# Reading values and gates from the projection's PSUM bank instead of from an SBUF copy

## The chip, the cores and the metric

The kernel runs on one core of a Trainium2 chip. The metric is the device time of one execution in microseconds (us), taken as the median of three runs. The engines are named as the profile names them: PE is TensorE's matmul, PEld its weight load, ACT is ScalarE, DVE is VectorE, POOL is GpSimd and SP the engine that issues the DMAs. SBUF is the on-chip working memory; PSUM holds the matmul results in banks of 512 float32 per partition. POOL does not read PSUM anywhere in this kernel, before or after.

## The reference

Two layers over x of 2048 frames by 1024 columns. Each layer normalizes x, makes one wide projection, splits its columns into q, k, v and gate g for two groups of heads, attends, multiplies each head's output by silu(g), concatenates, projects and adds the residual:

```python
z = rms_norm(x, ln_g) @ w_in
aq, ak, av, ag, bq, bk, bv, bg, bf = split_cols(z, EVEN_SPLITS)
aq = rms_norm(aq.reshape(bsz, seq, A_HEADS, 2, HEAD_DIM), a_qn_g)
...
mixed = jnp.concatenate([a_out * jax.nn.silu(ag), b_out * jax.nn.silu(bg)], axis=-1)
return x + mixed @ w_out
```

Layer 0 has A, four heads of differential attention over all earlier 64-frame chunks (two softmaxes, the second subtracted with a learned weight), and B, eight heads of causal attention with a forget bias. Layer 1 has C, eight query heads over two key-value heads in a window, and D, eight heads over the own and eight earlier chunks. Only q and k are RMS-normalized per head; v and g are used as the projection leaves them.

## The kernel before

The work is cut into steps. A step is one head unit and one block of 128 frames (tb, 0 to 15). The units follow one another: four units of A, four of B (each two heads), the output projection of layer 0, two units of C, four of D, the output projection of layer 1. In the trace these stages lie at about 0 to 780 us (A), 780 to 1430 (B), 1430 to 1620 (output projection), 1620 to 1990 (C, its first unit to 1820), 1990 to 2440 (D) and 2440 to the end.

One step of A, B or D does this:

- PE makes z, 128 frames by 512 columns (128 each of q, k, v, g), with 24 matmuls (`proj`, L242 to L244): eight blocks of the contraction, each as high x high, high x low and low x high of float16 pairs. z lies in one PSUM bank; the pool of these banks, `pz`, has two (`bufs` 2), shared by z, by C's key-value projection zk and by the output projections' zo.
- `evac` (L248) has ACT copy z into the SBUF tile zs, times a power of two held per partition in `sc`. Afterwards nothing reads the bank, and PE may fill it again, two projections later.
- `qk_prep` (L253) squares q and k (ACT, L258), sums (DVE, L260), takes the inverse root (`rstd`, L115: POOL L119 and the power on POOL L121, then DVE L123 to L125), scales q and k (DVE L266), applies k's gain (POOL L269), splits into float16 high and low parts (ACT L272, POOL L273). PE transposes them (L277, L281), ACT copies the results out as kT and qT (L283, L286).
- `v_split` (L289) multiplies zs's value columns by another power of two (POOL L294) and splits them: high part on ACT (L109), low part on POOL (L113).
- `silu2` (L308) takes tanh of the gate columns of zs on ACT (L313), forms (1 + tanh) x g on DVE (L314) and multiplies by a factor on POOL (L316, or L318 for A, where the factor is the row `subg`).
- QK products go to another PSUM pool (L339), DVE adds the bias and takes the running extreme (L351), ACT takes exp (L374), `weights_T` splits the weights (ACT L302, DVE L303), a DMA transposes them into pT, and PE multiplies them with V (L407; L497 for A). In A the second softmax is combined into the first by DVE (L484) and POOL (L481, L482).

In C's first unit a step makes two projections: zk with 256 columns (k and v, `post2`), then z with 512 (four heads of q, 256 gate columns). In its second unit a step makes only z.

Python code writes the pieces of a step in a merged order (`drive`): the projection of the step two ahead, the transposes of the step one ahead, QK of this one, the weighted sums of the last two. A scheduler then orders each engine's instructions over the whole program, so a change of a few instructions moves others too. Each engine works its queue strictly in that order: an instruction that waits holds up all that stand behind it.

Of the kernel before, what the change touches and what calls it, by code (L numbers as in the profile page):

```python
# [9 lines left out]
F32 = mybir.dt.float32  # L10
# [4 lines left out]
AF = mybir.ActivationFunctionType  # L15
ALU = mybir.AluOpType
AX = mybir.AxisListType

P = 128
# [40 lines left out]
class Trunk:  # L60
    def __init__(self, ctx, tc, t):
        self.ctx, self.tc, self.nc, self.t = ctx, tc, tc.nc, t
        nc = self.nc
        pool = lambda name, bufs, **k: ctx.enter_context(tc.tile_pool(name=name, bufs=bufs, **k))
        self.const = pool("const", 1)
        self.wp = pool("wp", 11)
        self.xp = pool("xp", 4)
        self.kvp = pool("kvp", 1)
        self.ap = pool("ap", 1)
        self.sm = pool("sm", 6)  # L70
        self.wsc = pool("wsc", 8)
        self.dram = pool("dram", 1, space=bass.MemoryType.DRAM)
        self.pz = pool("pz", 2, space=bass.MemoryType.PSUM)
        self.pS = pool("pS", 2, space=bass.MemoryType.PSUM)
        self.pT = pool("pT", 1, space=bass.MemoryType.PSUM)
        self.pO = pool("pO", 1, space=bass.MemoryType.PSUM)

        self.idf = self.const.tile([P, P], F32, name="idf")
        one = self.const.tile([P, 1], F32, name="one")
        nc.vector.memset(one[:], 1.0)  # L80
        nc.scalar.activation(one[:], one[:], AF.Exp)
        make_identity(nc, self.idf[:])
        self.lng = []
        for i in range(2):
            g = self.const.tile([P, KB], F32, name=f"lng{i}")
            nc.sync.dma_start(g[:], t[f"ln{i}"])
            self.lng.append(g)
        self.idh = self.const.tile([P, P], F16, name="idh")
        nc.vector.tensor_copy(self.idh[:], self.idf[:])
        self.onesf = self.const.tile([P, P], F32, name="onesf")  # L90
        nc.vector.memset(self.onesf[:], 1.0)
        self.mhalf = self.const.tile([P, 8], F32, name="mhalf")
        nc.vector.memset(self.mhalf[:], -0.5)

        def dt_(n, s):
            return [self.dram.tile(s, F32, name=f"{n}{b}") for b in range(NT)]

        self.xs = [[self.dram.tile([P, 2 * KB * P], F16, name=f"xs{i}_{b}") for b in range(NT)] for i in range(2)]
        self.xT = [[None] * NT for _ in range(2)]
        self.mix = [dt_("mixa", [P, DM]), dt_("mixb", [P, DM])]  # L100
        self.x1 = dt_("x1_", [P, DM])
        self.cumd = [self.dram.tile([8, 512], F32, name=f"cumd{i}") for i in range(4)]
# [143 lines left out]


    def evac(self, z, n, sc):  # L248
        zs = self.ap.tile([P, 512], F32, tag="zs", name="zs", bufs=3)
        self.nc.scalar.activation(zs[:, :n], z[:, :n], AF.Copy, scale=sc[:, 0:1])  # L250
        return zs

# [33 lines left out]
            nc.scalar.activation(qT[:].rearrange("p n a t -> p (n a) t"), pt[:, :2 * nq], AF.Copy)  # L286
            st["q"] = [qT[:, s] for s in range(nq)]

    def v_split(self, z, sc, heads):  # L289

        nc = self.nc
        V = self.kvp.tile([P, heads, 2, P // heads], F16, tag="V", name="V", bufs=19)
        z = z.rearrange("p (h d) -> p h d", h=heads)
        nc.gpsimd.tensor_scalar(out=z, in0=z, scalar1=sc[:, 1:2], scalar2=1.0, op0=ALU.mult, op1=ALU.mult)  # L294
        self.split(V[:, :, 0], V[:, :, 1], z, nc.scalar, nc.gpsimd)
        return V

    def weights_T(self, w, n, scale=PSC):
# [6 lines left out]
        nc.sync.dma_start_transpose(out=pt[:, :2 * n // P], in_=hl[:, :2 * n])  # L305
        return pt[:, :2 * n // P].rearrange("p (a b) q -> p a b q", a=2)

    def silu2(self, z, mul):  # L308

        nc = self.nc  # L310
        n = z.shape[1]
        g = self.ap.tile([P, n], F32, tag="gate", name="gate", bufs=7)
        nc.scalar.activation(g[:], z, AF.Tanh, scale=0.5)  # L313
        nc.vector.scalar_tensor_tensor(out=g[:], in0=g[:], scalar=1.0, in1=z, op0=ALU.add, op1=ALU.mult)  # L314
        if mul.shape[1] == 1:
            nc.gpsimd.tensor_scalar(out=g[:], in0=g[:], scalar1=mul, scalar2=1.0, op0=ALU.mult, op1=ALU.mult)  # L316
        else:
            nc.gpsimd.tensor_tensor(out=g[:], in0=g[:], in1=mul, op=ALU.mult)  # L318
        return g
# [106 lines left out]
    def unit_A(self, h, W, wsc, X):  # L426
        nc, ap = self.nc, self.ap
        ks, vs = [], []

        def mk(tb):  # L430
            st = {}
            m = tb + 1

            def p():
                def z():
                    if "z" not in st:
                        st["z"] = self.pz.tile([P, 512], F32, tag="z", name="z")
                    return st["z"][:]
                pieces = self.proj(st, z, W, 512)
                if h == 0:  # L440
                    pieces.append((KB * 0.056, lambda: self.forget(st)))

                def post():
                    z = self.evac(st["z"], 512, wsc())
                    kd = self.ktile(ks, tb)
                    g = self.qk_prep(st, z, 2, 2, self.gA[h], kd)
                    if h == 0:
                        self.forget_gate(st, tb)
                    next(g)
                    vs.append(self.v_split(z[:, 256:384], wsc(), 1))  # L450
                    st["gate"] = self.silu2(z[:, 384:512], self.subg[:])
                    next(g)
                    st["fin"] = g
                return pieces + [(0.34, post)]
# [62 lines left out]
    def unit_BD(self, kind, u, W, wsc, X):  # L517
        nc, ap = self.nc, self.ap
# [16 lines left out]
        def mk(tb):  # L535
            st = {}
# [3 lines left out]
            def p():  # L540
                def z():
                    if "z" not in st:
                        st["z"] = self.pz.tile([P, 512], F32, tag="z", name="z")
                    return st["z"][:]
                pieces = self.proj(st, z, W, 512)

                def post():
                    z = self.evac(st["z"], 512, wsc())
                    kd = self.ktile(ks, tb)
                    g = self.qk_prep(st, z, 2, 2, self.gB if kind == "B" else self.gD, kd)  # L550
                    next(g)
                    vs.append(self.v_split(z[:, 256:384], wsc(), 2))
                    st["gate"] = self.silu2(z[:, 384:512], wsc()[:, 2:3])
                    next(g)
                    st["fin"] = g
                    prep(tb)
                return pieces + [(0.34, post)]
# [46 lines left out]
    def unit_C(self, kv, W, wsc, Wkv, wsckv, KV, X):  # L604
# [6 lines left out]
        def mk(tb):  # L611
# [6 lines left out]
            def p():  # L618
                def zf(k):
                    if k not in st:  # L620
                        st[k] = self.pz.tile([P, 512], F32, tag="z", name="z")
                    return st[k]
                pieces = []
                if Wkv is not None:
                    def post2():
                        z2 = self.evac(st["zk"], 256, wsckv())
                        kd = self.ktile(ks, tb)
                        g = self.qk_prep(st, z2, 0, 2, self.gC, kd)
                        next(g)
                        vs.append(self.v_split(z2[:, 128:256], wsckv(), 2))  # L630
                        next(g)
                        st["fink"] = g
                    pieces = self.proj(st, lambda: zf("zk")[:, :256], Wkv, 256)
                    pieces.append((0.11, post2))

                def post():
                    z = self.evac(st["z"], 512, wsc())
                    g = self.qk_prep(st, z, 4, 0, self.gC, None, self.islope[:, 4 * kv:4 * kv + 4])
                    next(g)
                    st["gate"] = self.silu2(z[:, 256:512], usc[0]()[:, 2:3])  # L640
                    next(g)
                    st["fin"] = g
                return pieces + self.proj(st, lambda: zf("z")[:], W, 512) + [(0.45, post)]
# [271 lines left out]
    def run(self):  # L915
# [23 lines left out]
        def squares(key, kb, raw=None):  # L939

            src, n = parts(key, kb)
            if kb == 0:
                scales[key] = self.sm.tile([P, KB], F32, tag="wss", name="wss", bufs=2)
            g = gains(key)
            junk = raw
            if raw is None:
                raw = junk = self.wp.tile([P, 512], F32, tag="wrn", name="wrn", bufs=1)[:, :n]
                nc.sync.dma_start(raw, src)
            else:
                junk = self.ap.tile([P, 512], F32, tag="zs", name="junk", bufs=3)[:, :n]  # L950
            self.w_squares(scales[key][:, kb:kb + 1], raw, None if g is None else g[:, kb:kb + 1], junk)
            if kb == KB - 1:
                scales[key] = self.w_scale(scales[key][:], None if g is None else g[:])
# [187 lines left out]
```

## Time and profile before

| | |
|---|---|
| median of 3 runs | 2637.18 us (2636.54 to 2644.25) |
| the profiled execution's own time | 2638.93 us |
| its span, first to last instruction | 2637.2 us |
| mean granted PE clock | 0.961 |
| busy share: PE, DVE, ACT, POOL | 89%, 70%, 71%, 55% |

Busy is time in which an engine has an instruction running. Matmuls overlap, so PE's share overstates how near it is to its limit: a 128x512 matmul is shown with about 380 ns, but where PE is not held up the next one starts 215 ns later. "Idle before" counts what an engine stood still ahead of a kind of instruction, and names what it waited for. The times in a timeline are from the span's start.

### The profile page before, as it was taken

What the parts mean: (1) busy time and instruction counts of PE and PEld (TensorE: products, weight loads), DVE (VectorE), ACT (ScalarE), POOL (GpSimd) and SP (SyncE); (2) the same over time, 40 slices, a digit from 0 to 9 for tenths busy, and PEclk for the clock granted to TensorE, in tenths of its full rate; (3) what the DMA queues carried; (4) which work ended last, traced back from release to release, by engine and by line L of the source; (5) the groups of instructions that cost most, each with busy time, mean ns of one, the idle gap of its engine ahead of it and who ended that gap; (6) DMA issues with size and microseconds to landing.
All of it is one profiled execution on the core that took longest, in us unless ns stands there. A gap on an engine that the chain in (4) does not pass through costs nothing.

```text
span 2637.2 us, 53573 instructions
## 1 busy us (share of the span) xinstructions
PE 2345.4 (89%) x18560; PEld 1295.5 (49%) x18560; DVE 1851.6 (70%) x5212; ACT 1861.5 (71%) x4289; POOL 1453.8 (55%) x2311
## 2 busy tenths in 40 slices
PE   6779888989899989898986988999989999998899
PEld 3335444545455555455543434665555454555444
DVE  6877899798886867768676444666777676667431
ACT  6777677777777878778787444778888777777420
POOL 4647777786785645546463001756475757575300
PEclk9889999999999999999997999999999999999899
DMA  7875645355456997979789999345566676756982
GB/s 224 194 173 150 137 110 127 84 127 115 99 128 131 195 185 159 205 151 190 159 170 219 275 276 251 98 94 145 127 172 147 161 143 156 153 127 135 254 229 94
DMA packets 888208, 426.68 MB, mean 162 GB/s; under 512 B 785376, under 2 KB 816096, under 8 KB 887936
## 3 DMA queue, kind: packets, MB, share of 16 engines
q1 hardware_dynamic: 887936, 423.27, 70.1%
q8 instruction: 145, 2.38, 0.4%
q14 instruction: 127, 1.04, 0.1%
HBM read 187.68 MB, written 42.01 MB: 87 GB/s over the span
## 4 chain that ended last, share of the span: by engine, by line
PE 23%; DMA 13%; ACT 10%; DVE 9%; POOL 8%; issue 7%; SPq 1%; POOLq 0%; ACTq 0%; DVEq 0%
DMA pT<-ph 6%; PE z L242 3%; PE z L243 3%; PE z L244 3%; PE zo L242 2%; PE OT L407 2%; PE pss L339 2%; PE zo L243 2%; PE zo L244 2%; DVE row L351 2%; ACT ph L302 2%; POOL y L121 2%; DVE ph L303 2%; ACT row L374 2%; DMA wrn<-in_wd_dram 1%
## 5 line engine op out<-in xcount | busy, mean ns | idle before, releaser
L374 ACT ACTIVATE row<-row,mx 128x1024 f32<-128x1024 f32 (+7 forms) x512 | 438.2, 857 | 118.7 <-DVE mx L351 117.0
L339 PE MATMUL pss<-kT,qT 128*128 128x512 f16 (+3 forms) x1728 | 398.7, 347 | 50.4 <-DVE mx L351 38.9
L242 PE MATMUL z<-w,xr 128*128 128x512 f16 x896 | 346.7, 388 | 23.2 <-DMA xr<-xhl 14.0
L303 DVE SCALAR_TENSOR_TENSOR ph<-row,ph 128x1024 f16<-128x1024 f32 (+6 forms) x320 | 286.6, 905 | 106.2 <-ACT ph L302 104.8
L242 PE MATMUL z<-w,x 128*128 128x512 f16 x896 | 344.4, 384 | 7.1 <-DMA x<-xs 6.7
L243 PE MATMUL z<-w,xr 128*128 128x512 f16 x896 | 346.4, 387 | 3.8 <-POOL w L113 2.4
L244 PE MATMUL z<-w,xr 128*128 128x512 f16 x896 | 345.5, 386 | 0.0
L243 PE MATMUL z<-w,x 128*128 128x512 f16 x896 | 344.4, 384 | 0.0
L244 PE MATMUL z<-w,x 128*128 128x512 f16 x896 | 344.1, 384 | 0.0
L121 POOL TENSOR_TENSOR y<-v,mhalf 128x4 f32<-128x4 f32 (+2 forms) x329 | 306.5, 933 | 9.4
L407 PE MATMUL OT<-V,pT 128*128 128x64 f16 x5688 | 236.0, 196 | 82.5 <-DMA pT<-ph 79.4
L407 PEld LDWEIGHTS <-pT 128*128 128x128 f16 x5688 | 214.4, 100 | 149.5 <-DMA pT<-ph 104.1
L302 ACT ACTIVATE ph<-row 128x1024 f16<-128x1024 f32 (+6 forms) x320 | 234.3, 744 | 52.5 <-DMA pT<-ph 49.0
L339 PEld LDWEIGHTS <-qT 128*128 128x128 f16 x1728 | 153.3, 101 | 173.6 <-issue 58.5
L273 POOL TENSOR_TENSOR hl<-zs,hl 128x256 f16<-128x256 f32 (+1 forms) x240 | 179.9, 750 | 103.3 <-ACT hl L272 100.5
L123 DVE TENSOR_TENSOR q<-y 128x4 f32<-128x4 f32 (+2 forms) x329 | 92.3, 281 | 197.4 <-POOL y L121 195.5
L272 ACT ACTIVATE hl<-zs 128x512 f16<-128x512 f32 (+1 forms) x240 | 145.7, 608 | 54.4 <-POOL zs L269 47.9
L250 ACT ACTIVATE zs<-z,sc 128x512 f32<-128x512 f32 (+1 forms) x240 | 157.8, 660 | 33.9 <-PE z L244 33.4
L242 PE MATMUL zo<-w,xm 128*128 128x512 f16 x352 | 139.0, 395 | 29.3 <-DMA xm<-mhl 12.4
L242 PEld LDWEIGHTS <-xr 128*128 128x128 f16 x960 | 95.4, 99 | 117.3 <-DMA xr<-xhl 15.1
L113 POOL TENSOR_TENSOR w<-wraw,w 128x512 f16<-128x512 f32 x118 | 145.6, 1236 | 13.6 <-ACT w L109 12.6
L286 ACT ACTIVATE qT<-ptq 128x512 f16<-128x512 f16 (+1 forms) x224 | 144.8, 647 | 8.0 <-PE ptq L281 6.8
(223 smaller groups left out, 5489.1 us busy)
## 6 DMA issues: line engine op xcount, KB each, us to landing
x<-xs SPq DMA_DIRECT2D x112, 512.0 KB, 3.8
wraw<-in_w_dram SPq DMA_DIRECT2D x64, 256.0 KB, 3.0
wrn<-in_w_dram SPq DMA_DIRECT2D x56, 256.0 KB, 2.9
x<-in_x_dram SPq DMA_DIRECT2D x16, 512.0 KB, 4.9
xs<-xt SPq DMA_DIRECT2D x16, 512.0 KB, 3.3
mixa<-out SPq DMA_DIRECT2D x128, 64.0 KB, 2.2
biasB<-cumd SPq DMA_DIRECT2D x32, 256.0 KB, 4.6
wrn<-in_wo_dram SPq DMA_DIRECT2D x32, 256.0 KB, 3.0
```

Source lines behind the costliest of these rows:

```text
L121: nc.gpsimd.tensor_tensor(out=y[:], in0=v[:], in1=self.mhalf[:, :n], op=ALU.pow)
L242: nc.tensor.matmul(ps(), xh, wh, start=(kb == 0), stop=False)
L243: nc.tensor.matmul(ps(), xh, wl, start=False, stop=False)
L244: nc.tensor.matmul(ps(), xl, wh, start=False, stop=(kb == KB - 1))
L250: self.nc.scalar.activation(zs[:, :n], z[:, :n], AF.Copy, scale=sc[:, 0:1])
L272: nc.scalar.activation(hl[:, :, 0::2], zn[:, :, None, :].broadcast_to([P, n, 2, 64]), AF.Copy)
L273: nc.gpsimd.tensor_tensor(out=hl[:, :, 1], in0=zn, in1=hl[:, :, 0], op=ALU.subtract)
L302: nc.scalar.activation(hl[:, :n], w, AF.Copy, scale=scale)
L303: nc.vector.scalar_tensor_tensor(out=hl[:, n:2 * n], in0=w, scalar=scale, in1=hl[:, :n], op0=ALU.mult, op1=ALU.subtract)
L339: nc.tensor.matmul(ps, q()[:, j, :], k[:, slot, (b % 4) * P:(b % 4 + n) * P], start=(j == 0), stop=(j == 1 and not (end and diag)), skip_g ...
L374: nc.scalar.activation(row[:, :hm * P], row[:, :hm * P], AF.Exp, scale=-1.0, bias=nmax, accum_out=s[:, i:i + 1])
L407: nc.tensor.matmul(O[:, head], w()[:, a], V()[:, b], start=first and a + b == 0, stop=last and a == 1, skip_group_check=True)
```

## The change

`evac` copies only the q and k columns (256 of 512; 128 of 256 for zk). `v_split` reads the value columns from the PSUM bank: ACT writes the high part with a constant scale (L294), DVE subtracts it from the scaled PSUM values to give the low part (L295). POOL has no part in it any more. `silu2` reads the gate columns from the bank too: tanh takes its scale from `sc`, DVE's step reads PSUM, and the factor that evac used to apply goes into POOL's multiplication, which for A needs a small tile `subu` per unit, made once by POOL. The buffer `junk` of the first weight loads moves to the `row` pool, since zs is now half as wide.

```diff
     def evac(self, z, n, sc):
-        zs = self.ap.tile([P, 512], F32, tag="zs", name="zs", bufs=3)
+        zs = self.ap.tile([P, 256], F32, tag="zs", name="zs", bufs=3)
         self.nc.scalar.activation(zs[:, :n], z[:, :n], AF.Copy, scale=sc[:, 0:1])
...
-    def v_split(self, z, sc, heads):
+    def v_split(self, z, heads):
...
-        nc.gpsimd.tensor_scalar(out=z, in0=z, scalar1=sc[:, 1:2], scalar2=1.0, op0=ALU.mult, op1=ALU.mult)
-        self.split(V[:, :, 0], V[:, :, 1], z, nc.scalar, nc.gpsimd)
+        nc.scalar.activation(V[:, :, 0], z, AF.Copy, scale=2.0 ** -15)
+        nc.vector.scalar_tensor_tensor(out=V[:, :, 1], in0=z, scalar=2.0 ** -15, in1=V[:, :, 0], op0=ALU.mult, op1=ALU.subtract)
         return V
...
-    def silu2(self, z, mul):
+    def silu2(self, z, sc, mul):
...
-        nc.scalar.activation(g[:], z, AF.Tanh, scale=0.5)
+        nc.scalar.activation(g[:], z, AF.Tanh, scale=sc[:, 2:3])
         nc.vector.scalar_tensor_tensor(out=g[:], in0=g[:], scalar=1.0, in1=z, op0=ALU.add, op1=ALU.mult)
         if mul.shape[1] == 1:
-            nc.gpsimd.tensor_scalar(out=g[:], in0=g[:], scalar1=mul, scalar2=1.0, op0=ALU.mult, op1=ALU.mult)
+            nc.gpsimd.tensor_scalar(out=g[:], in0=g[:], scalar1=mul, scalar2=sc[:, 0:1], op0=ALU.mult, op1=ALU.mult)
...
# unit_A; B and D alike without subu
-                    z = self.evac(st["z"], 512, wsc())
+                    z = self.evac(st["z"], 256, wsc())
...
+                    if tb == 0:
+                        self.subu[h] = self.const.tile([P, P], F32, tag="subu", name="subu", bufs=2)
+                        nc.gpsimd.tensor_scalar(out=self.subu[h][:], in0=self.subg[:], scalar1=wsc()[:, 0:1], scalar2=1.0, op0=ALU.mult, op1=ALU.mult)
...
-                    vs.append(self.v_split(z[:, 256:384], wsc(), 1))
-                    st["gate"] = self.silu2(z[:, 384:512], self.subg[:])
+                    vs.append(self.v_split(st["z"][:, 256:384], 1))
+                    st["gate"] = self.silu2(st["z"][:, 384:512], wsc(), self.subu[h][:])
...
# the first weight loads
-                junk = self.ap.tile([P, 512], F32, tag="zs", name="junk", bufs=3)[:, :n]
+                junk = self.ap.tile([P, 512], F32, tag="row", name="junk", bufs=6)[:, :n]
```

Three places in the engines' queues, from the middle of the second unit of B and from the first unit of C. The numbers behind the names tell tiles apart, and the bracket lists the engines whose progress the instruction waits for. First ACT in B, before: the copy of a z, its square, its tanh, the value's high part.

```order
L250 ACTIVATE zs_14679<-z_14569,sc_10514 128x512 [waits PE_49]
L258 ACTIVATE sq_14681<-zs_14679 128x256 [waits Activation_49]
L313 ACTIVATE gate_14697<-zs_14679 128x128
L109 ACTIVATE V_14693<-zs_14679 128x2x64 [waits Pool_49]
L283 ACTIVATE kT_14526<-ptq_14621 128x2x128 [waits PE_49]
L286 ACTIVATE qT_14629<-ptq_14621 128x512
```

The same place of ACT's queue now:

```order
L250 ACTIVATE zs_14598<-z_14488,sc_10458 128x256 [waits PE_49]
L294 ACTIVATE V_14612<-z_14488 128x2x64
L258 ACTIVATE sq_14600<-zs_14598 128x256 [waits Activation_49]
L313 ACTIVATE gate_14615<-z_14488,sc_10458 128x128 [waits DVE_49]
L283 ACTIVATE kT_14446<-ptq_14540 128x2x128 [waits PE_49]
L286 ACTIVATE qT_14548<-ptq_14540 128x512
```

The value's high part now follows the copy at once and waits for nothing new; the tanh, which waited for no other engine, now waits for DVE. The copies kT and qT stand behind it as before.

DVE at the same step, before: the low parts of the weights of the step before, the sum of squares, a QK row, then the gate's step.

```order
L303 SCALAR_TENSOR_TENSOR ph_14455<-row_14452,ph_14455 128x896 [waits DMAHW6_49,Activation_49]
L303 SCALAR_TENSOR_TENSOR ph_14511<-row_14508,ph_14511 128x896 [waits DMAHW3_49,Activation_49]
L260 TENSOR_REDUCE ssq_14683<-sq_14681 128x4 [waits Activation_49]
L351 ISA row_14607,mx_14606<-pss_14573,biasB_13355,gBs_395 128x1024 [waits PE_49]
L351 ISA mx_14606 128x1
L314 SCALAR_TENSOR_TENSOR gate_14697<-gate_14697,zs_14679 128x128 [waits Activation_49]
```

DVE there now:

```order
L303 SCALAR_TENSOR_TENSOR ph_14431<-row_14428,ph_14431 128x896 [waits DMAHW5_49,Activation_49]
L295 SCALAR_TENSOR_TENSOR V_14612<-z_14488,V_14612 128x2x64 [waits PE_49,Activation_49]
L260 TENSOR_REDUCE ssq_14602<-sq_14600 128x4 [waits Activation_49]
L314 SCALAR_TENSOR_TENSOR gate_14615<-gate_14615,z_14488 128x128 [waits Activation_49]
L351 ISA row_14526,mx_14525<-pss_14492,biasB_13282,gBs_395 128x1024 [waits PE_49]
```

The value's low part is new in this queue, ahead of the sum of squares, and the gate's step has moved ahead of the QK row. Both now read the PSUM bank of z.

ACT in C's first unit, at the z of one step, before and then now:

```order
L250 ACTIVATE zs_24937<-z_24869,sc_22495 128x512 [waits PE_49]
L283 ACTIVATE kT_24664<-ptq_24888 128x2x128 [waits PE_49]
L258 ACTIVATE sq_24939<-zs_24937 128x256 [waits DVE_49,Activation_49]
L313 ACTIVATE gate_24952<-zs_24937 128x256
L669 ACTIVATE rowC_24821,stC_24822<-rowC_24821,stC_24822 128x256 [waits DVE_49]
```

```order
L250 ACTIVATE zs_24807<-z_24739,sc_22375 128x256 [waits PE_49,Pool_49]
L313 ACTIVATE gate_24822<-z_24739,sc_22375 128x256
L283 ACTIVATE kT_24536<-ptq_24758 128x2x128 [waits PE_49]
L258 ACTIVATE sq_24809<-zs_24807 128x256 [waits Activation_49]
L672 ACTIVATE rowC_24692,stC_24693<-rowC_24692,stC_24693 128x256 [waits DVE_49]
```

There the tanh has moved up to stand right behind the copy; this z has no value columns, so its tanh waits for no one.

More of the change, by code (lines that the diff above doesn't have):

```diff
@@ L82, in __init__ @@
         make_identity(nc, self.idf[:])
-        self.lng = []
+        self.lng, self.subu = [], {}
         for i in range(2):
@@ L547, in post @@
                 def post():
-                    z = self.evac(st["z"], 512, wsc())
+                    z = self.evac(st["z"], 256, wsc())
                     kd = self.ktile(ks, tb)
@@ L551, in post @@
                     next(g)
-                    vs.append(self.v_split(z[:, 256:384], wsc(), 2))
-                    st["gate"] = self.silu2(z[:, 384:512], wsc()[:, 2:3])
+                    vs.append(self.v_split(st["z"][:, 256:384], 2))
+                    st["gate"] = self.silu2(st["z"][:, 384:512], wsc(), wsc()[:, 2:3])
                     next(g)
@@ L625, in post2 @@
                     def post2():
-                        z2 = self.evac(st["zk"], 256, wsckv())
+                        z2 = self.evac(st["zk"], 128, wsckv())
                         kd = self.ktile(ks, tb)
@@ L629, in post2 @@
                         next(g)
-                        vs.append(self.v_split(z2[:, 128:256], wsckv(), 2))
+                        vs.append(self.v_split(st["zk"][:, 128:256], 2))
                         next(g)
@@ L636, in post @@
                 def post():
-                    z = self.evac(st["z"], 512, wsc())
+                    z = self.evac(st["z"], 256, wsc())
                     g = self.qk_prep(st, z, 4, 0, self.gC, None, self.islope[:, 4 * kv:4 * kv + 4])
                     next(g)
-                    st["gate"] = self.silu2(z[:, 256:512], usc[0]()[:, 2:3])
+                    st["gate"] = self.silu2(st["z"][:, 256:512], wsc(), usc[0]()[:, 2:3])
                     next(g)
```

## The prediction

> **What bounds the kernel now.** I read the page first, then busy time by stage, then who waited for whom, then the durations of the instructions that the change touches, and last the timeline around one reuse of a bank. The page's rows on the whole, with the chain that ended last:
>
> ```profile
> span 2637.2 us, 53573 instructions
> PE 2345.4 (89%) x18560; PEld 1295.5 (49%) x18560; DVE 1851.6 (70%) x5212; ACT 1861.5 (71%) x4289; POOL 1453.8 (55%) x2311
> PE 23%; DMA 13%; ACT 10%; DVE 9%; POOL 8%; issue 7%; SPq 1%; POOLq 0%; ACTq 0%; DVEq 0%
> ```
>
> No engine is full and the chain runs through all of them, so a stage has to be asked what limits it. The stages A (without its start), B, C's first unit and D, with columns PE, PEld, DVE, ACT, POOL, clock, DMA share, GB/s:
>
> ```profile
> 230.00:780.00 550.00, 482.08 (x3383) 269.96 (x3381) 480.93 (x1342) 412.48 (x982) 413.56 (x620) 0.97 0.50 117
> 780.00:1430.00 650.00, 574.75 (x5716) 330.93 (x5714) 489.67 (x1193) 513.75 (x1106) 361.79 (x565) 0.96 0.86 173
> 1620.00:1820.00 200.00, 184.95 (x1495) 115.52 (x1494) 121.00 (x401) 147.09 (x407) 117.75 (x198) 0.98 0.47 125
> 1990.00:2440.00 450.00, 424.40 (x3667) 238.74 (x3665) 311.32 (x882) 340.85 (x806) 293.96 (x508) 0.98 0.67 147
> ```
>
> In A, DVE is busy 481 of 550 us (87%), as much as PE is shown, and PE is not at its limit there; DVE comes nearest to bounding A. In B, PE, ACT (79%) and the DMA engines (0.86) are all close. C's first unit and D are PE's: 92% and 94%.
>
> Who waited for whom (us in all, times, longest us):
>
> ```profile
> DVE q L123 <- POOL y L121: 195.5, 169, 6.9
> PE OT L407 <- DMA pT<-ph: 79.4, 65, 5.2
> DVE ssq L260 <- ACT sq L258: 62.6, 60, 3.5
> ACT ph L302 <- POOL row L482: 30.2, 16, 3.1
> PE ptq L277 <- POOL hl L273: 22.4, 16, 4.3
> PE z L242 <- ACT zs L250: 2.2, 4, 0.7
> ```
>
> The last row says that PE hardly ever waits for a z bank today. The first says that DVE waits long for the power on POOL: 1.2 us each time, and the power itself takes 1064 ns (the first row below), so most of it is the power's own run and not a queue ahead of it.
>
> **The change, part by part.** The power, then the instructions removed, altered, and those that price the new ones (busy us in all, mean ns of one, idle before; the last gives least, median and most ns):
>
> ```profile
> L121 POOL TENSOR_TENSOR y<-v,mhalf 128x4 f32<-128x4 f32 x224 | 238.3, 1064 | 3.1
> L113 POOL TENSOR_TENSOR V<-zs,V 128x128 f16<-128x128 f32 x208 | 105.1, 507 | 57.6 <-ACT V L109 56.5
> L294 POOL TENSOR_SCALAR zs<-zs,sc 128x128 f32<-128x128 f32 x208 | 92.0, 443 | 100.8 <-ACT zs L250 97.8 <-PE ptq L281 1.5 <-PE pss L339 0.3
> L250 ACT ACTIVATE zs<-z,sc 128x512 f32<-128x512 f32 x224 | 150.6, 674 | 33.6 <-PE z L244 33.2 <-PE psf L741 0.3
> L250 ACT ACTIVATE zs<-z,sc 128x256 f32<-128x256 f32 x16 | 7.3, 457 | 0.2 <-PE z L244 0.2
> L109 ACT ACTIVATE V<-zs 128x128 f16<-128x128 f32 x208 | 61.6, 299 | 6.1 <-POOL zs L294 5.1
> L313 ACT ACTIVATE gate<-zs 128x128 f32<-128x128 f32 x192 | 57.1, 297 | 3.4 <-DVE out L508 3.4
> L505 ACT ACTIVATE out<-OA,cf 128x128 f32<-128x128 f32 x64 | 22.7, 354 | 9.6 <-PE OA L497 9.5
> L314 DVE SCALAR_TENSOR_TENSOR gate<-gate,zs 128x128 f32<-128x128 f32 x192 | 70.9, 370 | 0.4 <-ACT gate L313 0.4
> L411 DVE TENSOR_TENSOR out<-OT,gate 128x128 f32<-128x128 f32 x128 | 36.3, 284 | 16.0 <-PE OT L407 12.9 <-issue 1.2 <-POOL gate L316 1.0
> L351 DVE CUSTOM_DVE_ANT_0 row<-pss,distA,gA3s 128x1024 f32<-128x1024 f32 x72 | 91.8, 1276 | 17.8 <-PE pss L339 10.1 <-POOL row L482 7.3
> L727 DVE SCALAR_TENSOR_TENSOR res<-zo,mt,res 128x512 f32<-128x512 f32 x64 | 47.5, 748 | 86.7 <-PE zo L244 80.1 <-DMA res<-x 4.0 <-DMA res<-in_x_dram 2.6
> L484 DVE SCALAR_TENSOR_TENSOR row<-row,cf x96: 339/745/1659, 55.3 to 781.9; 128x512 f32<-128x512 f32 x72, 128x128 f32<-128x128 f32 x8, 128x256 f32<-128x256 f32 x8, 128x384 f32<-128x384 f32 x8
> ```
>
> *POOL.* It loses 208 x (0.507 + 0.443) = 197 us. How much of that lies on the path? The chain puts POOL at 8% of the span against 55% busy, so about 8/55 of a POOL microsecond counts: 29 us. Below, 0, if all of it hid (V is needed only by the weighted sums, steps later); above, 13.5% (197 of 1454) of all the waits for POOL shown, of which 0.135 x (195.5 + 30.2 + 22.4) = 34 us are the large ones. I take 29, the end nearer to the chain's own row. The four `subu` products cost 4 x about 0.44 us (L294's row) at most.
>
> *ACT.* The copy of 512 columns becomes one of 256: 224 x (0.674 - 0.457) = 49 us less; the 16 copies for zk, halved too, perhaps 2 more. The value's high part, from PSUM with a constant scale, stays near 299 ns. The tanh now takes its scale from memory and its input from PSUM; L505 does both on 128 columns in 354 ns: 192 x 0.057 = 11 us more. ACT's net is -40 us, and at the chain's 10% against 71% busy some 6 us count. Bounds: 0 and 40.
>
> *DVE.* 208 low parts are new. L411, with one PSUM input and 128 columns, puts one at 284 ns; the gate's step in its present mean, 370 ns, is the other end: 59 to 77 us. The gate's step itself, now with a PSUM input, should come down from 370 to L411's 284: 192 x 0.086 = 17 us less. Reading from PSUM adds nothing by itself: 512 columns take 748 ns from PSUM (L727) and a median 745 from SBUF (L484). Net +43 us, taking 284. In A, a third of the steps (64 of 208), it counts almost whole: 64 x (0.284 - 0.086) = 13; elsewhere 30 us x 9/70 = 4. Less POOL work also stretches DVE's SBUF steps less (L484's worst, 1659 ns, is more than twice its median), so I take 10. Bounds: 0 and 43.
>
> [...]
>
> *A new wait on ACT.* The tanh now waits for DVE (the order of ACT in B), and it does so until DVE has done the low part. Behind it stand the copies kT and qT, and the exps. One such place in A, ACT then DVE:
>
> ```profile
> 707.57 0.40 ACT L258 ACTIVATE sq<-zs 128x256 f32<-128x256 f32 x1
> 707.88 0.30 ACT L313 ACTIVATE gate<-zs 128x128 f32<-128x128 f32 x1
> 707.84 0.80 DVE L351 CUSTOM_DVE_ANT_0 row<-pss,distA,mx 128x512 f32<-128x512 f32 x1
> 708.64 0.40 DVE L260 TENSOR_REDUCE ssq<-sq 128x4 f32<-128x256 f32 x1
> ```
>
> ACT was done with the square at 707.97, DVE came to its sum at 708.64, 0.67 us late; the low part would stand there. The row of waits counts DVE early at this place 60 times out of 240, so it is late about 180 times: 180 x 0.67 = 121 us in which ACT would stand still. Of that, ACT's idle share (29%) covers part: 121 x 0.71 x 10/71 = 12 us. Bounds: 0 (the order puts other ACT work ahead of the tanh at many steps), and one long QK row of DVE each time (L351 above, 1276 ns), 180 x 1.28 = 230 us, 23 on the path.
>
> *The bank is held longer.* It used to be free once ACT had copied z; now the gate's step on DVE ends its use. Where PE comes back late this costs nothing. In C's first unit it comes back soon, since only zk stands between. Two cases there: the gate's step of one z and PE's next use of that bank; then the end of the next z, the first and last matmul of the zk behind it, PE's next use of the bank, and its gate's step:
>
> ```profile
> 1739.35 0.42 DVE L314 SCALAR_TENSOR_TENSOR gate<-gate,zs 128x256 f32<-128x256 f32 x1
> 1739.79 0.38 PE L242 MATMUL z<-w,xr 128*128 128x512 f16 x1
> ...
> 1745.93 0.38 PE L244 MATMUL z<-w,xr 128*128 128x512 f16 x1
> 1746.15 0.27 PE L242 MATMUL z<-wkv,x 128*128 128x256 f16 x1
> 1749.86 0.27 PE L244 MATMUL z<-wkv,x 128*128 128x256 f16 x1
> 1750.15 0.38 PE L242 MATMUL z<-w,x 128*128 128x512 f16 x1
> 1750.36 0.38 PE L243 MATMUL z<-w,x 128*128 128x512 f16 x1
> 1750.58 0.38 PE L244 MATMUL z<-w,x 128*128 128x512 f16 x1
> 1752.60 0.78 DVE L314 SCALAR_TENSOR_TENSOR gate<-gate,zs 128x256 f32<-128x256 f32 x1
> ```
>
> The first would just do (1739.77 before 1739.79). In the second, zk takes 4.0 us, and PE would stop from 1750.15 to 1753.38, 3.2 us. With 16 steps that is 0 to 51 us. The new order moves the tanh up behind the copy there, and a stopped PE lets ACT and DVE catch up; I take half a microsecond a step, 8 us. In A, B and D PE comes back a whole projection later, 24 matmuls at the 0.215 us of the last three PE rows, 5.2 us, and whatever stands between. The gate's step of 707.88 above was one in which DVE ran 0.67 us late, far inside that: I take nothing, and where DVE runs 5 us late the cover is gone and what is over 5 us is paid.
>
> *Junk in the row pool* touches the first 20 us, where x and weights are awaited: nothing, to 2 us either way.
>
> The sum: -29 - 6 + 10 + 12 + 8 = -5 us, against the profiled execution's 2638.9 (its span and 1.7 us around it), so 2634; that execution was 1.7 us above the median of the runs, which gives 2632.
>
> **The rivals.**
> *ACT and DVE in lockstep* (slower). The tanh's wait is not half covered but stands in B's chain of exp, split and transposition, at 17 us (121 x 10/71), and C's first unit loses half of the 3.2 us each time, 26 us; POOL's relief stays at 29, DVE costs 15 of its 17. Then -29 - 6 + 15 + 17 + 26 = +23: 2660 in terms of the median. For it speaks that A's DVE is late by design and that B's ACT is 79% busy; against it the ACT work that the order places ahead of the tanh. It decides from the point where DVE reaches the low part later than the end of ACT's square. [...]
>
> *POOL's waits shrink more* (faster). If the 248 us of waits for POOL shrink by 13.5% and what follows on DVE and PE moves up too, 34 us come on top of ACT's 6, with no new wait on the path: 2639 - 40 + 10 - 1.7 = 2607. For it: DVE's 195.5 us; against it: the power's own time makes up most of those.
>
> *Nothing moves* (the work removed was hidden). PE at 94% in D, DMA at 0.86 in B and the power's own time cover all: 2637.
>
> **How the numbers follow.** The forecast, a small gain, has a chance of 0.45 and reaches from 2612 to 2648, since the bounds of POOL's 0 to 34 and of the waits' 0 to 20 lie inside. Lockstep has 0.26, more from POOL 0.19, nothing 0.10. About 0.3% of the time, 8 us, is what a measurement of this kernel can tell from no change. Faster by more than that: 0.22 of the forecast's 0.45 and all of POOL's 0.19, 0.41. Within: 0.18 of the forecast, 0.01 of lockstep and the 0.10, 0.29. Slower: 0.05 and 0.25, 0.30. The range of 8 in 10 goes from 2600 to 2668: about half of each outer case's spread lies inside, one in ten is left out at either end.
>
> **What would show it.** In the profile after: POOL near 1257 us busy, ACT near 1820, DVE near 1895. The low part's row near 284 ns and the tanh's near 354; L313 with an idle time "<-DVE V" of under 120 us in all, or far more if lockstep holds. "PE z <- DVE gate" of about 8 us, at C's first unit, or 26 and more. DVE's wait for POOL's power down by some 20 us. The forecast is wrong if A is not shorter or no longer within 5 us, if B or C grow by over 10 us each, or if PE waits for banks in B or D.

## The result and the profile after

The changed kernel takes 2673.76 us (median of 4, 2668.46 to 2679.12) against 2640.72 us before on the same chip: a ratio of 1.0122, 95% interval 1.0099 to 1.0145. It is slower by 33 us, where a small gain was forecast. The page's first rows of the changed kernel:

```profile
span 2666.7 us, 53627 instructions
PE 2358.3 (88%) x18560; PEld 1305.9 (49%) x18560; DVE 1862.0 (70%) x5420; ACT 1817.4 (68%) x4289; POOL 1280.4 (48%) x1899
```

POOL lost 173 us of work, ACT 44, and DVE gained only 10, so each engine beside PE is freer or about as busy as before, and the program is longer. The groups of the changed steps, kept apart by shape:

```profile
L250 ACT ACTIVATE zs<-z,sc 128x256 f32<-128x256 f32 x224 | 103.5, 462 | 49.9 <-PE z L244 49.1 <-POOL gate L393 0.5
L294 ACT ACTIVATE V<-z 128x128 f16<-128x128 f32 x208 | 55.2, 268 | 4.5 <-PE OA L500 4.4
L295 DVE SCALAR_TENSOR_TENSOR V<-z,V 128x128 f16<-128x128 f32 x208 | 58.7, 285 | 48.7 <-ACT V L294 47.5 <-PE pss L339 0.3 <-PE OT L407 0.2
L313 ACT ACTIVATE gate<-z,sc 128x128 f32<-128x128 f32 x192 | 68.6, 362 | 17.2 <-DVE V L295 15.7
L314 DVE SCALAR_TENSOR_TENSOR gate<-gate,z 128x128 f32<-128x128 f32 x192 | 53.2, 279 | 11.2 <-ACT gate L313 10.0
```

The durations are those of the sum: 285 ns for the low part (284 taken), 362 for the tanh (354), 279 for the gate's step (284). The tanh's new wait for DVE is 15.7 us in all, not 121. Who waited for whom, in the changed kernel:

```profile
DVE q L123 <- POOL y L121: 166.7, 145, 6.8
PE pss L339 <- DVE mx L351: 57.1, 36, 5.0
PE z L242 <- DVE gate L314: 11.5, 10, 2.8
```

In the kernel before the second of these read:

```profile
PE pss L339 <- DVE mx L351: 38.9, 32, 3.7
```

DVE's wait for the power fell by 29 us (20 were named), and PE's waits for the gate's step to free a z bank are 11.5 us in all. None of these rows holds 33 us. So the next question is where the time was lost. Setting the end of each projection in the one trace beside that of the same projection in the other gives, in us that the changed kernel is late: -2 at the 17th of A's 64 projections, 1 at the 33rd, 7 at A's last, 38 at B's last, 31 at the start of C, 25 at the last of C's first unit, and 30 at the end of the program. All of it is lost in A and B, and C's first unit, the place that the prediction feared, is 7 us shorter. Within A and B it is lost at the start of each unit and partly won back at the end: blocks 3 to 9 of the units 2 to 8 (A's second to B's last; from the end of block 2's z to that of block 9) take 516 us in place of 469 in all, the six stretches between them 584 in place of 598.

One such stretch, A's fourth unit, PE in the changed kernel (some rows of the timeline; an entry with a count is a run of matmuls, the bracket is idle time before it and what ended it):

```profile
608.07 0.38 PE L244 MATMUL z<-w,xr 128*128 128x512 f16 x1
610.30 0.79 PE L339 MATMUL pss<-kT,qT 128*128 128x256 f16 x4 [1.29 <-DVE mx L351]
613.12 4.98 PE L500 MATMUL OA<-V,pT 128*128 128x128 f16 x45 [2.03 <-DMA pT<-ph]
624.50 1.74 PE L500 MATMUL OA<-V,pT 128*128 128x128 f16 x24 [3.32 <-DMA pT<-ph]
627.20 2.74 PE L500 MATMUL OA<-V,pT 128*128 128x128 f16 x24 [0.95 <-DMA pT<-ph]
630.37 0.63 PE L242 MATMUL z<-w,x 128*128 128x512 f16 x1
```

For 22 us PE has no projection in its queue. It works through QK and weighted sums alone and stands at each of them, with nothing to fill the wait. In the kernel before, the same z (block 5) begins 20 us earlier, right behind that of block 4; then the row of ACT at which the value's high part of block 3 is written, whose z had ended at 604.8:

```profile
608.96 0.38 PE L244 MATMUL z<-w,xr 128*128 128x512 f16 x1
609.73 0.38 PE L242 MATMUL z<-w,x 128*128 128x512 f16 x1
```

```profile
626.90 0.31 ACT L109 ACTIVATE V<-zs 128x128 f16<-128x128 f32 x1
```

And ACT in the changed kernel, where z of block 3 had ended at 601.4:

```profile
624.88 0.45 ACT L294 ACTIVATE V<-z 128x128 f16<-128x128 f32 x2 [2.32 <-PE OA L500]
```

The two rows of ACT say it. In both kernels V of block 3 is written 22 to 23.5 us after its z has ended, when a weighted sum (OA) of the unit before is done, for V has 19 buffers and a unit has 16 blocks: block 3 of a unit takes the buffer of block 0 of the unit before, which the last weighted sums of that unit still read. This holds in every unit from the second to the eighth: in the changed kernel V of block 3 is written 0.04 to 0.7 us after the end of the last matmul that reads the earlier V of its buffer. In the changed program of the fourth unit ACT's write of V waits for PE at blocks 3 and 4 and at no other block. Before, that delay hurt nobody, since zs held the values and the bank was free after ACT's copy. Now the bank itself holds the values, so the projection of block 5 can't begin before V of block 3 is written. PE never shows this as a long wait: the scheduler placed the projections behind those weighted sums.

### The profile page after: what moved, and what is told of

Read it like the earlier page. It is cut to its first block, busy times and chain, and to the rows that moved or that the text cites. A ratio compares the mean times of both kernels' runs of the same rounds, so it can differ in the third digit from the quotient of the medians.

```text
span 2666.7 us, 53627 instructions
## 1 busy us (share of the span) xinstructions
PE 2358.3 (88%) x18560; PEld 1305.9 (49%) x18560; DVE 1862.0 (70%) x5420; ACT 1817.4 (68%) x4289; POOL 1280.4 (48%) x1899
## 5 line engine op out<-in xcount | busy, mean ns | idle before, releaser
L339 PE MATMUL pss<-kT,qT 128*128 128x512 f16 (+3 forms) x1728 | 404.6, 349 | 66.2 <-DVE mx L351 57.1
L242 PE MATMUL z<-w,xr 128*128 128x512 f16 x896 | 346.8, 388 | 23.1 <-DMA xr<-xhl 9.2
L407 PE MATMUL OT<-V,pT 128*128 128x64 f16 x5688 | 241.7, 196 | 81.7 <-DMA pT<-ph 76.3
L407 PEld LDWEIGHTS <-pT 128*128 128x128 f16 x5688 | 219.8, 100 | 152.2 <-DMA pT<-ph 102.4
L272 ACT ACTIVATE hl<-zs 128x512 f16<-128x512 f32 (+1 forms) x240 | 146.5, 611 | 91.5 <-POOL zs L269 69.2
L119 POOL TENSOR_SCALAR v<-ssq 128x4 f32<-128x4 f32 (+1 forms) x240 | 61.3, 255 | 229.7 <-DVE ssq L260 190.0
L500 PE MATMUL OA<-V,pT 128*128 128x128 f16 x1632 | 127.6, 240 | 35.6 <-DMA pT<-ph 35.5
L170 POOL TENSOR_SCALAR wraw<-wraw,gs 128x512 f32<-128x512 f32 x128 | 106.0, 830 | 100.6 <-DMA wraw<-in_wo_dram 45.2
```

The source lines that it names most:

```text
L242: nc.tensor.matmul(ps(), xh, wh, start=(kb == 0), stop=False)
L272: nc.scalar.activation(hl[:, :, 0::2], zn[:, :, None, :].broadcast_to([P, n, 2, 64]), AF.Copy)
L339: nc.tensor.matmul(ps, q()[:, j, :], k[:, slot, (b % 4) * P:(b % 4 + n) * P], start=(j == 0), stop=(j == 1 and not (end and diag)), skip_g ...
L407: nc.tensor.matmul(O[:, head], w()[:, a], V()[:, b], start=first and a + b == 0, stop=last and a == 1, skip_group_check=True)
```

## The experiments

The theory that came to stand (it is theory 4 below) is that the z bank hangs on the ring of V buffers. Its rivals were the added work in DVE's queue (theory 1), the waits at the PSUM bank (theory 2), and the order as such (theory 3). All ratios are to the kernel before on the same chip; that one's median was 2651.5 to 2652.6 us in these runs, 0.4% above the 2640.72 us of the chip on which the result was measured, so times taken from traces of these runs stand some 0.4% high beside those above.

**Values alone.** From the kernel before, `v_split` of the change, the gate as it was:

```diff
-        nc.gpsimd.tensor_scalar(out=z, in0=z, scalar1=sc[:, 1:2], scalar2=1.0, op0=ALU.mult, op1=ALU.mult)
-        self.split(V[:, :, 0], V[:, :, 1], z, nc.scalar, nc.gpsimd)
+        nc.scalar.activation(V[:, :, 0], z, AF.Copy, scale=2.0 ** -15)
+        nc.vector.scalar_tensor_tensor(out=V[:, :, 1], in0=z, scalar=2.0 ** -15, in1=V[:, :, 0], op0=ALU.mult, op1=ALU.subtract)
```

> The values from PSUM (high part on ACT, low part on DVE), the gate as before from the SBUF copy, which stays 512 columns wide. Theory 1, DVE's queue: the low part on DVE, ahead of the sum of squares and of the QK rows, makes PE wait for DVE's rows in B and in A's second half, and the relief of POOL is worth nothing; the changed kernel's +33 us come with this half alone: 2660 to 2675 (1.008 to 1.013), 'PE pss <- DVE mx' near 57 us in all against 39 before. Theory 2, the PSUM source: the gate's wait and the bank held for it cost; then the values alone give under 2645. Theory 3, the order: any edit that makes the scheduler place the program anew moves the time by up to 30 us either way, without regard to what is edited.

Measured: 1.0113 (1.0098 to 1.0128), with "PE pss <- DVE mx" at 60.6 us. The loss comes with the values. As theory 1 expected, but theory 4 expects it too.

**Gates alone.** From the changed kernel, the values as before from a zs of 384 columns:

```diff
-                    z = self.evac(st["z"], 256, wsc())
+                    z = self.evac(st["z"], 384, wsc())
...
-                    vs.append(self.v_split(st["z"][:, 256:384], 2))
+                    vs.append(self.v_split(z[:, 256:384], wsc(), 2))
```

> The gate from PSUM, the values as before from the SBUF copy (384 columns), split by ACT and POOL. Theory 1: 2630 to 2642 (0.996 to 1.001), since DVE gets no new instruction. Theory 2: 2655 and more. Theory 3: anything within 30 us.

Measured: 1.0033 (1.0022 to 1.0044): a little above theory 1's range and far below theory 2's. The kernel has the change's new place for the junk too, whose own ratio follows below, so the gate's part can't be told from nothing.

**The low part on DVE, but from SBUF.** From the kernel before:

```diff
-        nc.gpsimd.tensor_scalar(out=z, in0=z, scalar1=sc[:, 1:2], scalar2=1.0, op0=ALU.mult, op1=ALU.mult)
-        self.split(V[:, :, 0], V[:, :, 1], z, nc.scalar, nc.gpsimd)
+        nc.scalar.activation(V[:, :, 0], z, AF.Copy, scale=sc[:, 1:2])
+        nc.vector.scalar_tensor_tensor(out=V[:, :, 1], in0=z, scalar=sc[:, 1:2], in1=V[:, :, 0], op0=ALU.mult, op1=ALU.subtract)
```

> The kernel before, with the value's high part taken by ACT from the SBUF copy in one step with its scale and the low part taken by DVE from the SBUF copy; no PSUM bank is held longer, POOL is relieved of the same 197 us. Theory 1: slower like the changed kernel, 2655 to 2680 (1.006 to 1.015). Theory 2: under 2645. Theory 3: anything within 30 us.

Measured: 0.9995 (0.9985 to 1.0004). Theory 1 falls: the same work on the same engines costs nothing while the bank is not held for it. DVE even has more to do here than in the changed kernel (1898.8 us against 1862.0, the low part taking 396 ns in the mean against 285), and "PE pss <- DVE mx" is 40.9 us.

**Junk alone.** From the kernel before:

```diff
-                junk = self.ap.tile([P, 512], F32, tag="zs", name="junk", bufs=3)[:, :n]
+                junk = self.ap.tile([P, 512], F32, tag="row", name="junk", bufs=6)[:, :n]
```

> The kernel before with only the buffer of the first weight loads in another pool: no instruction differs in kind or size, but the scheduler places the whole program anew. Theories 1 and 2: 2637 to 2645, no change. Theory 3: a change of 10 us or more either way.

Measured: 1.0045 (1.0030 to 1.0060), 12 us, as theory 3 expected, for an edit that touches the first 20 us only. Beside the trace of the kernel before this one falls behind bit by bit (7 us at the 17th projection, 10 at A's last, 29 at C's first), but the two traces are of different chips, so where the edit's own 12 us lie is not shown. So a new order by itself can be worth some 0.45%, and effects of that size can't be put down to an edit by one kernel. It is too little for the whole loss.

**The kernel before in the new order of PE, and the new steps in the old order.** The matmuls of one kernel are tied, each to the one ahead of it, in the order that the other kernel has:

```diff
+        for n, d in enumerate(steps):
+            at, was = at + d, at
+            if n:
+                self.tc.add_manual_dep(ins[at], ins[was].name, info, reason="order")
```

> The kernel before, every instruction as it was, but TensorE's queue is tied to the order in which the changed kernel has it (the scheduler places the other engines around it). Theory 3, the order, now stated for TensorE's queue: the loss is in that order, which has less work between a z and its QK (21.2 us of matmuls in the mean of B against 24.3) and between QK and the weighted sum in A (20.1 against 21.7); then this is slower by 0.8 to 1.3%. Theory 2, the PSUM source and its waits: nothing of them is here, so within 0.3% of before.

Measured: 1.0309 (1.0288 to 1.0330), more than the changed kernel itself, although no instruction is new and PE's wait for a bank is 3.4 us:

```profile
PE z L242 <- ACT zs L250: 3.4, 2, 3.1
```

> The changed kernel with TensorE's queue tied to the order that the kernel before has, and 21 buffers for V in place of 19 (with 19 that order would lock up: a z bank now comes free only when a V buffer does, and in the old order the z stands ahead of the weighted sum that frees it). Theory 3: the loss is gone, 0.990 to 1.002, and what is left is the worth of the changed steps themselves. Theory 2: still slower by 0.8% or more, with 'PE z <- DVE gate' far above the changed kernel's 11.5 us.

Measured: 1.0108 (1.0088 to 1.0128). Theory 3's expectation missed: the loss is not gone. Theory 2's came true, ratio and wait: PE now stands before the banks instead:

```profile
PE z L242 <- DVE gate L314: 70.7, 32, 5.9
```

An order made for one set of steps can be bad for another, so tying is a blunt tool. In the first of the two PE's wait for POOL before the transposes ("PE ptq <- POOL hl") is 89.1 us, against 22.4 in the kernel before and 21.5 in the changed kernel: it has a cost that the changed kernel hasn't, and its 1.0309 can't be read as the price of the order there. What they do show: an order of PE can cost this much with none of the new waits; and in the old order PE waits 71 us for banks that are held longer, 51 of them in A and B, where the prediction saw none.

**The changed kernel with 21 buffers for V.**

```diff
-        V = self.kvp.tile([P, heads, 2, P // heads], F16, tag="V", name="V", bufs=19)
+        V = self.kvp.tile([P, heads, 2, P // heads], F16, tag="V", name="V", bufs=21)
```

> The changed kernel with 21 buffers for V and nothing tied. The order that the scheduler gives TensorE then lies between the two: 21.3 us between QK and the weighted sum in A, 22.9 us between z and QK in B. Theory 3: 1.003 to 1.009, a part of the loss. Theory 2: 1.010 to 1.014, as the changed kernel.

Measured: 0.9968 (0.9956 to 0.9979). Two buffers of 512 bytes a partition take away the whole loss, more than theory 3 expected, and theory 2's range is missed; the gain of 0.32% that is left is within what a new order alone can do. Here theory 4 was formed. At the place shown above, in this kernel, PE has the next projection 5 us behind the last, and ACT writes V of block 3 while that block's successor is still in work:

```profile
596.79 0.38 PE L244 MATMUL z<-w,xr 128*128 128x512 f16 x1
602.13 0.38 PE L242 MATMUL z<-w,x 128*128 128x512 f16 x1
```

```profile
595.19 0.27 ACT L294 ACTIVATE V<-z 128x128 f16<-128x128 f32 x1
```

The stretch from the end of block 3's z to that of block 9's in that unit, as window and length, busy us of PE, PEld, DVE, ACT and POOL, granted clock, DMA share and GB/s: before, changed, changed with 21 buffers.

```profile
604.80:654.30 49.50, 45.65 (x336) 25.85 (x334) 43.40 (x145) 37.10 (x100) 34.27 (x59) 1.00 0.50 111
```

```profile
601.40:664.90 63.50, 55.36 (x381) 32.87 (x377) 46.81 (x166) 40.68 (x109) 38.84 (x57) 0.89 0.42 95
```

```profile
591.10:648.10 57.00, 51.69 (x372) 29.66 (x370) 51.46 (x175) 45.20 (x117) 37.68 (x59) 0.97 0.50 105
```

**The changed kernel with the junk in a buffer of its own.**

```diff
-                junk = self.ap.tile([P, 512], F32, tag="row", name="junk", bufs=6)[:, :n]
+                junk = self.wp.tile([P, 512], F32, tag="jnk", name="junk", bufs=1)[:, :n]
```

> The changed kernel with the first weight loads' junk in a buffer of its own, so that the row pool is as before. If the junk's +0.45% adds to the rest, 1.006 to 1.010; if the order that each edit happens to get decides, anything from 1.004 to 1.014, and by its TensorE order, which is like the changed kernel's (20.3 us in A, 22.0 in B), 1.009 to 1.012.

Measured: 1.0143 (1.0125 to 1.0161), just above all three ranges; only the widest, with its end at 1.014, lies partly inside the interval. The junk's 0.45% does not come off; it was the scatter of one order, no price that adds to others.

**Three trials of the ring.** The values alone with 21 buffers, the kernel before with 21, the changed kernel with 17 and with 23; the edit is the one number each time.

> The values alone from PSUM (the first experiment), with 21 buffers for V in place of 19. Theory 4, the ring of V: a z bank comes free only when the value's parts are written, and these wait for a V buffer, which at the third and later blocks of each unit is held by the unit before until its last weighted sums; so the scheduler moves z back, behind those sums. Then two more buffers take the loss away here as in the changed kernel: 0.993 to 1.002 against 1.0113 with 19. Theory 3, the order as a lottery: any new order draws from about 0.995 to 1.015 without regard to the buffers, so anything in there.

Measured: 1.0018 (1.0004 to 1.0031), against 1.0113 with 19. As theory 4 expected, though theory 3's range holds it too.

> The kernel before with 21 buffers for V. Theory 4: no z bank hangs on V here, so there is nothing to win: 0.996 to 1.005, a new order's own scatter. If the two buffers were worth 1.5% by themselves, 0.985.

Measured: 1.0011 (0.9997 to 1.0025). Nothing to win where no bank hangs on V, though V of blocks 3 and 4 is now written 8 us after the z's end in the mean, not 20.

> The changed kernel with 17 buffers for V in place of 19. Theory 4: the bank hangs on the ring from the first block of a unit on, and the loss grows: 1.020 to 1.045 against 1.0122 with 19. Theory 3: 0.995 to 1.015.

Measured: 1.0278 (1.0258 to 1.0299). As theory 4 expected, and outside theory 3's range; the gap moves as well, to the blocks that theory 4 names (below).

> The changed kernel with 23 buffers for V; with more than these the order no longer changes, so the ring doesn't bind any more. Theory 4: 0.992 to 0.999, as with 21 (0.9968). Theory 3: 0.995 to 1.015.

Measured: 0.9966 (0.9954 to 0.9978), as with 21: the ring binds no more.

What ties these together is one quantity of the traces: from the end of a z to the first matmul of the z two blocks later, which takes the same bank. Means over the units 2 to 8, blocks 3 and 4; and the sum of blocks 3 to 9 of these units, as above (the first two rows are from the one chip, the others from the chips that take 0.4% longer, 2 us of 469):

```
kernel                              gap, us   blocks 3-9, us   ratio
before                                 10.2              469   1
changed (19 buffers for V)             23.1              516   1.0122
values alone, 19                       21.5              503   1.0113
gates alone, 19                         8.8              478   1.0033
low part on DVE from SBUF, 19           9.5              470   0.9995
junk alone, 19                          9.1              470   1.0045
before in the new order of PE          24.0              522   1.0309
new steps in the old order, 21         10.6              473   1.0108
changed, 21                            12.1              459   0.9968
changed, junk apart, 19                23.3              508   1.0143
values alone, 21                       10.8              467   1.0018
before, 21                              9.6              470   1.0011
changed, 17                             5.6              565   1.0278
changed, 23                            12.6              459   0.9966
```

Every kernel with 19 buffers in which V is written from the bank has the gap, and none of the others has it but the one that was given the order. With 17 buffers the gap moves: blocks 1 and 2 have 44.5 and 38.7 us (means over the same units), blocks 3 and 4 have 6, just as 16 blocks and one spare buffer would have it. The new steps in the old order have no gap and lose outside these blocks; the 70.7 us of waits for banks are what their rows show for it.

## Why the prediction was wrong

**What bounds A and B.** It was right that no engine is full and that the chain runs through all. That PE has spare time in A did not protect it. What PE needs there is something to do while attention's chain of DVE, ACT and DMA runs, and the projections are that filler.

**POOL, -29 us.** POOL fell by 173 us of the 197. The three waits for it that the prediction added up fell from 248 to 208 us, where its bound took 34 us off; but ACT's wait for k's gain ("ACT hl L272 <- POOL zs L269"), which it left out, rose from 47.9 to 69.2. What the relief is worth can only be bounded: the kernel that moves the low part to DVE from SBUF takes the same work from POOL and ends at 0.9995, so POOL's relief and the extra load of DVE (47 us) and ACT (16) cancel there to within some 4 us, apart from the scatter of orders. By the prediction's own terms (-29, and for DVE 64 x 0.284 + 41 x 0.13 = 23) it would have won 6.

**ACT, -6, and DVE, +10.** The durations were right to within 3%, but for the value's high part, 268 ns where 299 was taken. DVE's busy time rose by 10 us rather than 43. Of the rest, 19 us are the two small steps behind the power on POOL (L124 from 244 to 221 ns in the mean, L125 from 245 to 210); no run tests the prediction's reason, less stretching by POOL, but for these steps the two traces fit it: L124 took at most 165 ns in its 187 cases with no POOL instruction beside it and 356 in the mean in the other 142, and in the changed kernel at most 166 in 210 cases and 333 in 119. L484, which it named, got longer (785 to 836). With the ring out of the way (23 buffers) the change gains 0.34%, 9 us; the whole sum said 5. That agreement is within the scatter of orders and no proof of each term.

**The new wait of the tanh, +12.** It was 15.7 us of waiting in all, where 121 were feared; the order places other ACT work ahead, as the prediction's lower bound had it. ACT and DVE in lockstep, the rival that forecast 2660, had the right sign by the wrong cause.

**The bank held longer, +8: the step that failed.** The prediction looked for its price in C's first unit, where next to none shows: that stage got shorter, 177 us in place of 184 from its first projection to the last, and PE's waits for the gate's step there are 1.4 us. The windows of that stage, before and changed, and the wait:

```profile
1631.00:1815.00 184.00, 169.93 (x1416) 107.69 (x1414) 114.16 (x378) 135.11 (x376) 114.78 (x192) 0.98 0.46 118
```

```profile
1662.00:1839.00 177.00, 167.38 (x1416) 107.42 (x1414) 114.26 (x406) 129.34 (x381) 95.27 (x160) 0.99 0.49 123
...
PE z L242 <- DVE gate L314: 1.4, 1, 1.4
```

For the rest it said: "In A, B and D PE comes back a whole projection later", "I take nothing". It took one place in A where DVE ran 0.67 us late for the rule (its row of 707.88 is the tanh; the gate's step behind it is not shown there), and asked only how late DVE might run. What it left out is that the writer of V must also have somewhere to write. The places of ACT's queue shown ahead of it in B lie in the middle of a unit, where that writer waits for nothing new. The trace of before had it: V of blocks 3 and 4 of the units 2 to 8 is written 20.3 us in the mean after the end of its z, and the next z took that bank 10.2 us after it. Any mean or median over all steps hides these 14 of 128. With the change the later of the two sets the earlier: in the order the gap is 23.1 us, blocks 3 to 9 are 47 us longer, and 14 of that come back in the six stretches between. Of the signs named in advance B's length showed it: A's last weighted sum ends 2 us later than before and B's last 30 us, so that B grew by 28 us where 10 were to count against the forecast.

**Where it is paid.** In blocks 3 to 9 of the units 2 to 8 PE stands still for 71 us in place of 46, and the granted clock is 0.5 for 58 us in place of 24. At that clock the z matmuls start 0.43 us apart (the median in both traces), in place of 0.215, so half of the 34 us more is lost, as an estimate, and the two make 25 + 17 = 42 of the 47 us. With 17 buffers they are 105 and 133 us, with 23 they are 41 and 21. Over the whole trace PE's waits for QK's banks grew ("PE pss <- DVE mx" 57.1 us, 39 before); those for transposed weights (OA and OT together) are 112 us in both kernels. In the stretch shown the granted clock is 0.5 from 612.0 to 618.8 and from 625.6 to 632.5, 0.89 in the mean, against 1.00 before. The first z matmuls after it are shown with 0.63 us in place of 0.38. The first fall, at 612.0, comes after a stop of 1.29 us and within one of 2.03; the second, at 625.6, comes 1.1 us after the end of one of 3.32. What length of stop brings the clock down is not shown.

**The junk, nothing to 2 us.** Alone it cost 12 us, by a new order; in the changed kernel its share can't be read off.

What stays open: whether the 0.32% and 0.34% with 21 and 23 buffers are the worth of the change or the scatter of an order, how they would divide among the halved copy, the gate's step and POOL, and why tying PE to a foreign order costs as much as 3%.

## What to carry to other kernels

Before a copy out of PSUM is removed, list everything that its readers wait for, the buffers they write into among them: the copy's reader may wait on a ring without harm, but a reader of the bank makes the producer wait for that ring. Look for this in the tail and by place (the first blocks of a unit), not in a median over steps, and read the order as well as the waits, since the scheduler here turned such a wait into a worse order that no row of waits shows. When the dependence is found, one or two more buffers may be the whole cure: here 2 x 512 bytes a partition turned 1.0122 into 0.9968.

## What the runs showed of the hardware

POOL's gate product over 128 columns got slower when its second scalar came from memory instead of being the constant 1.0: 425 ns in the mean before, 545 in the changed kernel, where the least time of the line is 432 ns against 365. With the values alone, where the constant stayed, the mean is 427 ns; with the gates alone it is 502 and in the changed kernel with 21 buffers 525, where it did not. The line's medians over both widths, 372 and 374 against 448, 442 and 447, differ less, so part of the mean's growth lies in long single cases. The rows of the kernel before and of the changed one:

```profile
L316 POOL TENSOR_SCALAR gate<-gate,sc 128x128 f32<-128x128 f32 x128 | 54.4, 425 | 9.3
L316 POOL TENSOR_SCALAR gate<-gate,sc x160: 365/372/1563, 742.5 to 2432.0; 128x128 f32<-128x128 f32 x128, 128x256 f32<-128x256 f32 x32
```

```profile
L316 POOL TENSOR_SCALAR gate<-gate,sc 128x128 f32<-128x128 f32 x128 | 69.7, 545 | 15.4 <-DVE gate L314 5.9 <-DVE q L123 2.9 <-DVE q L124 1.7
L316 POOL TENSOR_SCALAR gate<-gate,sc x160: 432/448/1877, 752.7 to 2468.5; 128x128 f32<-128x128 f32 x128, 128x256 f32<-128x256 f32 x32
```

That is 15 us of the 24 by which POOL's saving fell short of 197.

The gate's step on DVE over 128 columns had a mean of 370 ns with both inputs in SBUF and of 279 with one of them in PSUM, but its median hardly moved, from 282 to 279 ns. With the values alone from PSUM, where the gate's step still read SBUF, the mean is 360; with the gates alone it is 280. So the gain is in the long cases (up to 1193 ns before, over all widths, and 423 in the changed kernel), and not in the usual one.
